# A two-layer hybrid transformer on one core: the residual stream kept with tokens on the partitions

## The chip, the cores and the metric

The kernel runs on one core of one Trainium2 chip. The metric is the device time of one execution in microseconds (us). A core has TensorE (PE in the rows; its weight loads are PEld), VectorE (DVE), ScalarE (ACT), GpSimd (POOL) and SyncE (SP), which here only issues DMAs. Each engine works through its own queue in order.

## The reference, cut to what matters

Two layers work on a residual `h` of 256 tokens by 2048 features, in float32. Each layer adds three branches to it: a mixer (two kinds of sparse attention in layer 0, a retention in layer 1), a cross-attention over 256 memory tokens, and a gated feed-forward of width 5632 with a short convolution. Every branch reads a normalised copy of `h` and ends in an output projection.

```python
for l in range(DEPTH):                       # DEPTH = 2
    hn = _rmsnorm(h, norm_mix[l])
    h = h + (_mixer_ab(hn, ...) if l % 2 == 0 else _mixer_c(hn, ...))   # ends in "@ w_out", K = 2048 and 4096
    h = h + _cross_attn(_rmsnorm(h, norm_cross[l]), mem_n, w_q[l], w_kv[l], w_o[l])   # "@ w_o", K = 512
    h = h + _conv_ffn(_rmsnorm(h, norm_ffn[l]), w_up[l], conv_w[l], conv_b[l], w_down[l])   # "@ w_down", K = 5632
return _rmsnorm(h, norm_final)

def _rmsnorm(x, g):
    return x * rsqrt(mean(x * x, axis=-1) + eps) * g
```

## The kernel before

**Numbers.** A float32 product is made of three matmuls in the fast float32 format: each operand is split in a high part and the rest (`hi` and `lo` of a weight, left and right half of an x tile), and hi·hi, hi·lo and lo·hi are summed in PSUM. `weights` (L225 to L239) loads 512 KB of a weight into one of 4 `raw` tiles (DMA on SP's queue), ScalarE makes `hi` (L235), VectorE makes `lo` (L236); a *slab* is 128 rows of the contraction.

**Two forms of product.** `product_b` (L241 to L287) holds the weights stationary and streams x: per slab and 128 output features one matmul over 512 columns (L275: hi times both halves of x) and one over 256 (L280: lo times x's high half). The result has features on the partitions and tokens along the row. `product_a` (L307 to L328) holds x stationary and streams the weights: per slab and 128 tokens three matmuls over the weight's columns (L323 to L325); the result has tokens on the partitions. `product_n` (L294 to L305) is the first form with three matmuls of 256 columns into a smaller PSUM tile; it serves the output projection of the cross-attention.

**The residual** lies with features on the partitions: `hT[s]` (L342 to L343), 16 tiles of 128 features by 256 tokens. All output projections use the first form in blocks of 256 features. `residual` (L595 to L604) adds a block's PSUM to `hT` with two VectorE additions (L598, L600) for each 128 features. In a branch's last projection `feed` (L345 to L349) at once makes that slab of the next branch's x (ScalarE L200, VectorE L203) and adds the slab's squares to a running sum (ScalarE L150, VectorE L151). The norm's scale per token follows from that sum: two tiny matmuls (L172), some 13 tiny VectorE operations (L178 to L189) and a broadcast by two matmuls (L196). The scale is applied behind the next branch's first products, so these do not wait for it.

**Order.** Engine queues are laid out by a scheduler from the order of the program, but where `manual_schedule` names TensorE, its queue is the program's order word for word. That holds for the mixer of layer 0, the cross-attention up to `w_o`, and the retention's heads. `run` advances generators that each yield after a few slabs and calls `pump`, which advances the generators in `side` (attention heads, the norm's scale, the memory's preparation) by one step.

**The end.** `final` (L1051 to L1061) scales each 128 features, turns them to tokens by two TensorE transposes (L1060) and copies them out; the last norm's scale is applied before the store.

Of the kernel before, what the change touches and what calls it, by code (L numbers as in the profile page):

```python
# [12 lines left out]
F32 = mybir.dt.float32  # L13
# [4 lines left out]
ALU = mybir.AluOpType  # L18
# [16 lines left out]
for _name, _n in (("mix", 32), ("cross", 32), ("mem", 16), ("ffn", 32), ("final", 16), ("gn", 32), ("pe_k", 32),  # L35
                  ("pe_v", 32), ("conv0", 352), ("conv1", 352)):
    PAR[_name] = (PAR_END, PAR_END + _n)
    PAR_END += _n


def cols(c0, c1, n):
# [34 lines left out]
def hybrid_kernel(ctx: ExitStack, tc: tile.TileContext, a, out):  # L76
# [61 lines left out]
    class Norm:  # L138


        def __init__(self):
            self.acc = None

        def add(self, h):
            if self.acc is None:
                self.acc = new([P, S], F32, "nacc", 2)
                act.activation(self.acc, h, AF.Square)
            else:
                sq = work()
                act.activation(sq, h, AF.Square)  # L150
                dve.tensor_add(self.acc, self.acc, sq)  # L151

        def row_steps(self):

            self.r = new([P, S], F32, "rstd", 2)
            yield
            yield
            self.c = rsqrt_col(self.acc, D)
            yield
            yield  # L160
            act.activation(self.r, on_rows(self.c), AF.Copy)

        def row(self):
            for _ in self.row_steps():
                pass
            return self.r
# [127 lines left out]
    def product_n(w, xs, c0, evac):  # L294

        b = bank()
        n = len(xs)
        ws = list(weights(w, 0, n, c0, 2 * P))
        for j in range(2):
            o, c = b[:, j * S : (j + 1) * S], slice(j * P, (j + 1) * P)  # L300
            for k, (hi, lo) in enumerate(ws):
                xh, xl = xs[k][:, 0:S], xs[k][:, S:]
                pe.matmul(o, hi[:, c], xh, start=(k == 0), stop=False)  # L303
                pe.matmul(o, hi[:, c], xl, start=False, stop=False)  # L304
                pe.matmul(o, lo[:, c], xh, start=False, stop=(k == n - 1))  # L305
        for j in range(2):
            evac(j, b[:, j * S : (j + 1) * S])  # L307

# [4 lines left out]
    def product_a_steps(w, xs, c0, ncol, evac):  # L313
        ws = weights(w, 0, len(xs), c0, ncol)
        acc = acc_tile()
        n = len(xs)
# [28 lines left out]
    def feed(norm, xs, g):  # L345
        def f(s):
            xs.append(xhat(hT[s], g[:, s : s + 1]))
            norm.add(hT[s])
        return f  # L349
# [3 lines left out]
    xs_mix = []  # L353
    held = [[], []]
# [10 lines left out]
    with tc.manual_schedule(engines=engines):  # L365
# [5 lines left out]
        for i in range(5):  # L371
            if i < 4:
# [8 lines left out]
                for k in range(4):  # L381
# [3 lines left out]
                    xhat_hi(xs_mix[s], hT[s], g)  # L385
# [3 lines left out]
                    xhat_lo(xs_mix[s], hT[s], g)  # L389
# [24 lines left out]
    def setup_steps():  # L414
# [7 lines left out]
        load_par(pool, "conv0", "conv1")  # L422

# [109 lines left out]
    def cross(l, xs, norm, head_done):  # L533
        region = ExitStack()
        region.enter_context(tc.manual_schedule(engines={mybir.EngineType.PE}))
# [19 lines left out]
        run(*[product_b_steps(weights(w_q, 0, ND, 2 * P * blk, 2 * P), xs, ev_q) for blk in range(2)])  # L555
# [5 lines left out]
        os, vs = [None] * 4, {}  # L561

        def head(h):
# [9 lines left out]
            while h // 2 not in vs:  # L573
                yield
            v, c = vs[h // 2], h % 2 * P
            o = bank()
            for kb in range(2):
                pe.matmul(o[:, 0:S], v[:, kb, c : c + P], pt[:, kb * S : (kb + 1) * S], start=(kb == 0), stop=(kb == 1))
# [5 lines left out]
        for blk in range(2):  # L584
            v = long().rearrange("p (t c) -> p t c", t=2)
            product_a(w_kv, xm, 512 + blk * 2 * P, 2 * P,
                      lambda t, acc: act.activation(v[:, t, :], acc, AF.Copy, scale=mem_rms[1][:, t : t + 1]), n=4)
            vs[blk] = v
        while side:
            pump(4)  # L590
        region.close()
# [259 lines left out]
    def ffn(l, xs, norm, done):  # L851
        row = norm.row()
# [3 lines left out]
        def convolved(acc, j):  # L856
# [6 lines left out]
            dve.tensor_mul(u[:, 2:], t, row)  # L863
# [6 lines left out]
        def up(s0, n):  # L870
            os = []
            for pair in range(n // 2):
# [14 lines left out]
                product_b(w_up, xs, j0 * P, ev_gate)  # L887
# [13 lines left out]
    def mixer_c(xs, norm, done):  # L901
        row, col = norm.row(), norm.c
# [3 lines left out]
        dve.tensor_mul(cos_r, cos_l[1], row)  # L906
        dve.tensor_mul(sin_r, sin_l[1], row)
# [15 lines left out]
        def head(h):  # L923
# [6 lines left out]
            def ev_v(t, acc):  # L930
                sm = small(1)
                act.activation(v[t], acc, AF.Identity, scale=col[:, t : t + 1], accum_out=sm)
# [7 lines left out]
            def ev_g(j, acc):  # L940
                u = work()
                into(u, acc, row)
# [56 lines left out]
        for hp in range(RET_HEADS // 2):  # L999
            with tc.manual_schedule(engines={mybir.EngineType.PE}):  # L1000
                os = head(2 * hp) + head(2 * hp + 1)
# [5 lines left out]

    n_cross = Norm()
    xs_c = []
# [10 lines left out]
    def mix_out(blk, os):  # L1020
        w = Weight("w_out_ab", D)
        ws = chain(weights(w, 8, 8, blk * 2 * P, 2 * P), weights(w, 0, 8, blk * 2 * P, 2 * P))
        return product_b_steps(ws, os, residual(2 * blk, fc), n=ND)

    with tc.manual_schedule(engines={mybir.EngineType.PE}):
        os = Ordered(*mixer_ab(xs_mix, row, col, kcv))
        fc = feed(n_cross, xs_c, gain("cross"))
        run(mix_out(0, os), mix_out(1, os))
    assert not side
    side.extend((angle_steps(1), mem_rms_steps()))  # L1030
    for blk in range(2, ND // 2):
        run(mix_out(blk, os))

    n_ffn = Norm()
    xs_f = []
    cross(0, xs_c, n_cross, feed(n_ffn, xs_f, gain("ffn")))
    n_mix = Norm()
    xs_m = []
    ffn(0, xs_f, n_ffn, feed(n_mix, xs_m, gain("mix")[:, ND:]))

    n_cross = Norm()
    xs_c = []
    mixer_c(xs_m, n_mix, feed(n_cross, xs_c, gain("cross")[:, ND:]))
    n_ffn = Norm()
    xs_f = []
    cross(1, xs_c, n_cross, feed(n_ffn, xs_f, gain("ffn")[:, ND:]))


    n_fin = Norm()
    fin = {}  # L1050

    def final(s):
        n_fin.add(hT[s])
        y = work()
        act.activation(y, hT[s], AF.Copy, scale=gain("final")[:, s : s + 1])
        b = bank()
        for t in range(2):
            if s % 4 == 0:
                fin[t, s // 4] = new([P, 512], F32, "xs", 32)
# [93 lines left out]
```

## Time and profile before

| what | value |
|---|---|
| median of 3 runs | 2885.48 us (2885.35 to 2887.01) |
| the profiled execution, its own time | 2888.33 us |
| its span, first to last instruction | 2886.6 us |
| TensorE busy | 2850.2 us, 99% of the span, 16434 matmuls |
| VectorE, ScalarE busy | 2095.7 us (73%), 1492.1 us (52%) |
| mean DMA rate | 183 GB/s, 527 MB in all |
| granted TensorE clock, mean | 0.996 |

The span is 1.7 us shorter than the execution's own time, and that time lies 2.85 us above the median of the runs. Matmuls overlap, so a row's mean duration is not what one costs: the distance between two starts is. In the rows of the timeline the columns are start, length, engine, line, operation, tiles and shape, count, and in brackets the idle time of the engine before it and what ended it.

### The profile page before, as it was taken

Reading aid. Unit: us, or ns where it says so; the run is one execution under the profiler, and the core shown is the slowest. Engines: PE = TensorE matmul, PEld = TensorE weight load, DVE = VectorE, ACT = ScalarE, POOL = GpSimd, SP = SyncE. Lnnn points to the kernel's source line nnn. Section 1 sums busy time; section 2 is a strip of 40 time slices with the busy share of each in tenths; the row PEclk is TensorE's granted clock in tenths of the full one; section 3 lists DMA queues with packets and bytes.
Section 4 is the critical chain, followed back from the end, with each engine's and each line's share of the span. In section 5 each row is a group of like instructions: output and inputs, shape, how many; then the busy total and the mean of one; then the engine's idle time right before and its main releaser. Section 6 shows DMA issues by size and latency. Waiting matters only on the chain.

```text
span 2886.6 us, 43866 instructions
## 1 busy us (share of the span) xinstructions
PE 2850.2 (99%) x16434; PEld 2508.4 (87%) x16434; DVE 2095.7 (73%) x3785; ACT 1492.1 (52%) x2274; POOL 27.1 (1%) x203
## 2 busy tenths in 40 slices
PE   9999999999999999999999999999999999999998
PEld 8888888988888888888888888888898888888886
DVE  7766786877777777786666667668777777777775
ACT  5344555654555455454444444445565454545555
POOL 0000000000000000000000000000000000000000
PEclk9999999999999999999999999999999999999999
DMA  8434555555555555655555555555555556565553
GB/s 283 155 124 139 170 194 186 175 190 184 183 194 190 187 190 192 192 189 177 179 182 180 187 177 183 175 180 188 190 173 189 187 180 196 188 191 189 189 188 123
DMA packets 155957, 527.26 MB, mean 183 GB/s; under 512 B 16928, under 2 KB 25536, under 8 KB 155744
## 3 DMA queue, kind: packets, MB, share of 16 engines
q1 hardware_dynamic: 154464, 521.55, 55.3%
q8 instruction: 129, 2.11, 0.3%
q0 software_dynamic: 704, 1.85, 0.2%
q10 hardware_dynamic: 576, 1.05, 0.1%
q14 instruction: 84, 0.69, 0.1%
HBM read 522.29 MB, written 2.10 MB: 182 GB/s over the span
## 4 chain that ended last, share of the span: by engine, by line
PE 93%; DVE 3%; DMA 1%; ACT 1%; issue 1%; SPq 0%; ACTq 0%; DVEq 0%
PE acc L275 51%; PE acc L280 26%; PE acc L323 3%; PE acc L325 3%; PE acc L324 3%; DVE t L236 1%; PE bank L964 0%; PE bank L675 0%; PE bank L479 0%; PE bank L303 0%; PE bank L305 0%; PE bank L304 0%; DMA t<-in_w_out_ab_dram 0%; PE bank L499 0%; PE bank L491 0%
## 5 line engine op out<-in xcount | busy, mean ns | idle before, releaser
L275 PE MATMUL acc<-t,t 128*128 128x512 f32 x6784 | 1645.0, 393 | 10.3 <-DVE t L203 6.5
L275 PEld LDWEIGHTS acc<-t,t 128*128 128x128 f32 x6784 | 1246.0, 189 | 252.6 <-DVE t L203 7.0
L235 ACT ACTIVATE t<-t 128x1024 fp32r<-128x1024 f32 x978 | 1018.0, 1042 | 817.1 <-PE acc L275 513.1
L236 DVE TENSOR_TENSOR t<-t,t 128x1024 fp32r<-128x1024 f32 x978 | 1174.8, 1203 | 352.0 <-ACT t L235 342.8
L280 PEld LDWEIGHTS acc<-t,t 128*128 128x128 f32 x6784 | 877.0, 191 | 42.0 <-DVE t L236 4.1
L280 PE MATMUL acc<-t,t 128*128 128x256 f32 x6784 | 897.2, 284 | 6.0 <-DVE t L236 3.6
L598 DVE TENSOR_TENSOR t<-t,acc 128x256 f32<-128x256 f32 x272 | 113.2, 416 | 108.0 <-PE acc L275 107.3
L323 PE MATMUL acc<-t,t 128*128 128x512 f32 (+2 forms) x512 | 181.6, 355 | 0.4 <-DVE t L335 0.4
L859 ACT ACTIVATE t<-acc 128x256 f32<-128x256 f32 x176 | 65.9, 374 | 220.1 <-PE acc L275 220.1
L325 PE MATMUL acc<-t,t 128*128 128x512 f32 (+2 forms) x512 | 179.3, 350 | 0.0
L324 PE MATMUL acc<-t,t 128*128 128x512 f32 (+2 forms) x512 | 179.2, 350 | 0.0
L862 DVE TENSOR_TENSOR t<-acc,t 128x256 f32<-128x256 f32 x176 | 74.1, 421 | 144.5 <-ACT t L859 144.5
L865 ACT ACTIVATE t<-t,t 128x256 f32<-128x256 f32 x176 | 106.0, 602 | 41.5 <-DVE t L863 41.2
L600 DVE TENSOR_TENSOR t<-t,acc 128x256 f32<-128x256 f32 x272 | 113.1, 416 | 4.1
L333 ACT ACTIVATE t<-acc 128x256 f32<-128x256 f32 x112 | 42.5, 380 | 133.2 <-PE acc L275 130.6
L323 PEld LDWEIGHTS acc<-t,t 128*128 128x128 f32 x512 | 96.8, 189 | 13.3 <-PE acc L280 0.5
L325 PEld LDWEIGHTS acc<-t,t 128*128 128x128 f32 x512 | 96.8, 189 | 12.6
L324 PEld LDWEIGHTS acc<-t,t 128*128 128x128 f32 x512 | 96.9, 189 | 12.2
L335 DVE TENSOR_TENSOR t<-acc,t 128x256 f32<-128x256 f32 x112 | 46.8, 418 | 66.1 <-ACT t L333 66.1
L867 DVE SCALAR_TENSOR_TENSOR t<-t,t,t 128x256 f32<-128x256 f32 x176 | 84.4, 479 | 2.8
L866 DVE SCALAR_TENSOR_TENSOR t<-t,t,t 128x256 f32<-128x256 f32 x176 | 84.2, 478 | 2.4 <-ACT t L865 1.5
L863 DVE TENSOR_TENSOR t<-t,t 128x256 f32<-128x256 f32 x176 | 74.4, 423 | 3.0
(195 smaller groups left out, 1396.1 us busy)
## 6 DMA issues: line engine op xcount, KB each, us to landing
t<-in_w_up_dram SPq DMA_DIRECT2D x352, 512.0 KB, 3.5
t<-in_w_in_c_dram SPq DMA_DIRECT2D x192, 512.0 KB, 3.7
t<-in_w_down_dram SPq DMA_DIRECT2D x160, 512.0 KB, 3.5
t<-in_w_in_ab_dram SPq DMA_DIRECT2D x83, 512.0 KB, 3.6
t<-in_w_out_c_dram SPq DMA_DIRECT2D x64, 512.0 KB, 3.6
t<-in_w_out_ab_dram SPq DMA_DIRECT2D x32, 512.0 KB, 4.4
t<-in_w_kv_x_dram SPq DMA_DIRECT2D x32, 512.0 KB, 4.1
t<-in_w_q_x_dram SPq DMA_DIRECT2D x16, 512.0 KB, 4.4
```

Of the source, the lines that this page charges most:

```text
L235: act.activation(hi[:, 0 : m * ncol], raw[:, 0 : m * ncol], AF.Copy)
L236: dve.tensor_sub(lo[:, 0 : m * ncol], raw[:, 0 : m * ncol], hi[:, 0 : m * ncol].bitcast(F32))
L275: pe.matmul(acc[:, j, :], parts[k - k0][0][:, j * P : (j + 1) * P], xs[k], start=(k == 0), stop=(end and k == n - 1))
L280: pe.matmul(acc[:, j, 0:S], parts[k - k0][1][:, j * P : (j + 1) * P], xs[k][:, 0:S], start=False, stop=(end and k == n - 1))
L323: pe.matmul(o, xh, hi, start=(k == 0), stop=False)
L324: pe.matmul(o, xh, lo, start=False, stop=False)
L325: pe.matmul(o, xl, hi, start=False, stop=(k == n - 1))
L598: dve.tensor_add(h, h, acc[:, 0:S])
L600: dve.tensor_add(h, h, acc[:, S:])
L865: act.activation(c, u[:, 2:], AF.Identity, bias=cp[:, 3, j : j + 1], scale=cp[:, 2, j : j + 1])
L866: dve.scalar_tensor_tensor(c, u[:, 1 : S + 1], cp[:, 1, j : j + 1], c, op0=ALU.mult, op1=ALU.add)
L867: dve.scalar_tensor_tensor(c, u[:, 0:S], cp[:, 0, j : j + 1], c, op0=ALU.mult, op1=ALU.add)
```

## The change

1. The residual is held with tokens on the partitions: `res[t]`, two tiles of 128 tokens by 2048 features, loaded from a second copy of the input (`rows`, 2 MB) by two DMAs on SP's queue. The first norm still reads the input with features on the partitions, whose tiles now come from the pool `long`.
2. All output projections use the second form (x stationary) over 512 columns, and so does the value projection of the cross-attention, which had 256. `product_n` is gone. A group of 512 output features has one addition for each 128 tokens.
3. A norm's squares are summed by ScalarE's accumulating output (8 numbers per token), so VectorE's running sum and the two tiny matmuls go.
4. Where a group is final, a generator `turn(g)` goes into `side`: two steps later it transposes the group's 4 slabs by 8 TensorE transposes and makes the next x from PSUM.
5. The end needs no transposes: it multiplies by the gain laid out along the row (`gains`, 4 DMAs on POOL's queue).
6. TensorE's queue is the program's order from the first mixer to the end; the scales of the norms before the feed-forward and the retention become `side` steps.

```diff
 WIDTHS = {
...
-    "w_kv_x": cols(0, 1024, 256),
-    "w_out_ab": cols(0, D, 256),
-    "w_out_c": cols(0, D, 256),
-    "w_o_x": cols(0, D, 256),
-    "w_down": cols(0, D, 256),
+    "w_kv_x": cols(0, 512, 256) + [(512, 512)],
+    "w_out_ab": cols(0, D, 512),
+    "w_out_c": cols(0, D, 512),
+    "w_o_x": cols(0, D, 512),
+    "w_down": cols(0, D, 512),
 }
...
         def __init__(self):
-            self.acc = None
-
-        def add(self, h):
-            if self.acc is None:
-                self.acc = new([P, S], F32, "nacc", 2)
-                act.activation(self.acc, h, AF.Square)
-            else:
-                sq = work()
-                act.activation(sq, h, AF.Square)
-                dve.tensor_add(self.acc, self.acc, sq)
+            self.sq = new([P, 8], F32, "sq", 2)
+
+        def add(self, t, g):
+            junk = new([P, 512], F32, "p", 7)
+            act.activation(junk, part(t, g), AF.Square, accum_out=self.sq[:, 4 * t + g : 4 * t + g + 1])
+
+        def column(self):
+            v = small(2)
+            dve.tensor_reduce(v, self.sq.rearrange("p (t i) -> p t i", t=2), axis=AX.X, op=ALU.add)
+            self.c = rsqrt_of(v, D)
+            return self.c
...
-    x_in = [new([P, 2, S]) for _ in range(ND // 2)]
-    hT = [x_in[s // 2][:, s % 2, :] for s in range(ND)]
+    res = [new([P, D]) for _ in range(2)]
+
+    def part(t, g):
+        return res[t][:, 512 * g : 512 * g + 512]
+
+    def feed(norm, xs, gains):
+        def turn(g):
+            yield
+            yield
+            for s in range(4 * g, 4 * g + 4):
+                b = bank()
+                for t in range(2):
+                    pe.transpose(b[:, t * P : (t + 1) * P], res[t][:, s * P : (s + 1) * P], ident)
+                xs[s] = xhat(b[:, 0:S], gains[:, s : s + 1])
+
+        def f(g):
+            for t in range(2):
+                norm.add(t, g)
+            side.append(turn(g))
...
+        for t in range(2):
+            nc.sync.dma_start(res[t], a["rows"][t * P : (t + 1) * P, :])
...
-        for blk in range(ND // 2):
-            product_n(w_o, os, blk * 2 * P, residual(2 * blk, head_done))
-
-    def residual(s0, done=None):
-        def ev(j, acc):
-            h = hT[s0 + j]
-            dve.tensor_add(h, h, acc[:, 0:S])
-            if acc.shape[-1] > S:
-                dve.tensor_add(h, h, acc[:, S:])
-            if done is not None:
-                done(s0 + j)
+        out_product(w_o, os, 0, head_done)
+
+    def residual(g, done=None):
+        def ev(t, acc):
+            dve.tensor_add(part(t, g), part(t, g), acc)
+            if t and done is not None:
+                done(g)
         return ev
 
     def out_product(w, xs, s0, done=None):
-        for blk in range(ND // 2):
-            product_b(w, xs, blk * 2 * P, residual(2 * blk, done), s0=s0)
+        for g in range(4):
+            run(product_a_steps(w, xs, 512 * g, 512, residual(g, done), s0=s0))
...
     def ffn(l, xs, norm, done):
-        row = norm.row()
+        side.append(norm.row_steps())
...
+        def final(g):
+            for t in range(2):
+                norm.add(t, g)
+                ys[t, g] = new([P, 512], F32, "xs", 32)
+                dve.tensor_mul(ys[t, g], part(t, g), gains[g])
```

How the queues move shows at three places. **SP's queue near the start** (t is a tile, `in_w_in_ab` the first mixer's weights, `in_cmp_w_k` a table that the first mixer needs later). Before:

```order
L234 DMA t_383<-in_w_in_ab_dram 128x1024
L234 DMA t_442<-in_w_in_ab_dram 128x1024
L656 DMA t_513<-in_cmp_w_k_dram 128x4x128
L656 DMA t_515<-in_cmp_w_k_dram 128x4x128
L656 DMA t_517<-in_cmp_w_k_dram 128x4x128
L234 DMA t_473<-in_w_in_ab_dram 128x1024
```

Now:

```order
L229 DMA t_385<-in_w_in_ab_dram 128x1024
L229 DMA t_444<-in_w_in_ab_dram 128x1024
L421 DMA t_72<-in_rows_dram 128x2048
L421 DMA t_73<-in_rows_dram 128x2048
L229 DMA t_477<-in_w_in_ab_dram 128x1024
L646 DMA t_517<-in_cmp_w_k_dram 128x4x128
```

The two loads of `rows`, 1 MB each, stand ahead of that product's third and fourth weight loads; the fourth follows the eighth table load, as it did before.

**TensorE's queue where the cross-attention ends and the feed-forward begins** (bank is a PSUM bank, t_72 and t_73 the residual, t_61 the identity, acc_5210 the first product of `w_up`). Before, the last row of `w_o` and the first of `w_up` were neighbours:

```order
L305 MATMUL bank_5516<-t_5198,t_5519 128x256
L275 MATMUL acc_5588<-t_5234,t_5590 128x512 x2
L275 MATMUL acc_5588<-t_5240,t_5590 128x512 x2
L275 MATMUL acc_5588<-t_5278,t_5590 128x512 x2
L275 MATMUL acc_5588<-t_5285,t_5590 128x512 x2
```

Now the last group's transposes stand between the second and the third four slabs of `w_up`:

```order
L270 MATMUL acc_5210<-t_5139,t_5256 128x512 x2
L337 MATMUL bank_5277<-t_61,t_72 128x128
L337 MATMUL bank_5277<-t_61,t_73 128x128
L337 MATMUL bank_5283<-t_61,t_72 128x128
L337 MATMUL bank_5283<-t_61,t_73 128x128
L337 MATMUL bank_5289<-t_61,t_72 128x128
L337 MATMUL bank_5289<-t_61,t_73 128x128
L337 MATMUL bank_5295<-t_61,t_72 128x128
L337 MATMUL bank_5295<-t_61,t_73 128x128
L270 MATMUL acc_5210<-t_5188,t_5302 128x512 x2
```

So a group has two steps of the next product (32 matmuls, 16 of each length) between its last matmul and its transposes, and the x made of it is read one step (16 matmuls) behind them.

**VectorE's queue where the first cross-attention begins** (t_4378 is the fourth load of memory features, t_4388 and the like the weights of `w_q`). Before, twelve of the sixteen L203 rows on the memory stood ahead of the norm's scale (L178):

```order
L203 SCALAR_TENSOR_TENSOR t_4484<-t_4473,t_71,t_4484 128x256
L178 TENSOR_SCALAR t_4454<-bank_4451 128x2
L236 TENSOR_TENSOR t_4489<-t_4487,t_4488 128x1024
L180 TENSOR_SCALAR t_4456<-t_4454 128x2
L203 SCALAR_TENSOR_TENSOR t_4511<-t_4509,t_71,t_4511 128x256
```

Now twelve stand behind the scale and behind the last group's x (L198 on a bank):

```order
L184 SCALAR_TENSOR_TENSOR t_4224<-t_4235,t_4224 128x2
L198 SCALAR_TENSOR_TENSOR t_4279<-bank_4276,t_71,t_4279 128x256
L198 SCALAR_TENSOR_TENSOR t_4285<-bank_4282,t_71,t_4285 128x256
L198 SCALAR_TENSOR_TENSOR t_4291<-bank_4288,t_71,t_4291 128x256
L198 SCALAR_TENSOR_TENSOR t_4297<-bank_4294,t_71,t_4297 128x256
L198 SCALAR_TENSOR_TENSOR t_4302<-t_4300,t_71,t_4302 128x256
```

Eleven more such rows follow, then the `lo` of the fifth weight load of `w_q` (L231), which TensorE reads 32 matmuls of each length, eight transposes and two broadcasts after the last group.

## Rows read from the trace of the kernel before

**Rows 1.** The page's part 4, the chain that ended last.
```profile
PE 93%; DVE 3%; DMA 1%; ACT 1%; issue 1%; SPq 0%; ACTq 0%; DVEq 0%
```
**Rows 2.** Timeline of TensorE in a stretch of products with stationary weights.
```profile
847.92 3.82 PE L275 MATMUL acc<-t,t 128*128 128x512 f32 x16
...
853.49 3.82 PE L275 MATMUL acc<-t,t 128*128 128x512 f32 x16
```
**Rows 3.** Timeline of TensorE in a value product of the retention, x stationary.
```profile
1367.41 0.39 PE L323 MATMUL acc<-t,t 128*128 128x512 f32 x1
...
1373.54 0.39 PE L323 MATMUL acc<-t,t 128*128 128x512 f32 x1
```
**Rows 4.** Timeline of TensorE in the cross-attention's output projection.
```profile
513.25 0.28 PE L303 MATMUL bank<-t,t 128*128 128x256 f32 x1
...
514.33 0.28 PE L303 MATMUL bank<-t,t 128*128 128x256 f32 x1
```
**Rows 5.** Timeline of TensorE around six transposes of attention weights.
```profile
341.74 0.82 PE L479 MATMUL bank<-t,t 128*128 128x128 f32 x6
342.31 2.09 PE L275 MATMUL acc<-t,t 128*128 128x512 f32 x8
```
**Rows 6.** Windows: the last projection's stretch with transposes, for L275, then for L280.
```profile
2828.40:2871.60 43.20, 27.07 (x105) 18.61 (x104) 1.00 0.28 88
...
2828.40:2871.60 43.20, 18.04 (x112) 15.51 (x111) 1.00 0.28 88
```
**Rows 7.** Timeline of TensorE around a norm's tiny matmuls.
```profile
1333.09 0.50 PE L172 MATMUL bank<-t,t 128*128 128x1 f32 x4
1333.45 0.72 PE L275 MATMUL acc<-t,t 128*128 128x512 f32 x2
```
**Rows 8.** Timeline of TensorE: its long waits outside the feed-forward, and what followed.
```profile
349.53 0.78 PE L280 MATMUL acc<-t,t 128*128 128x256 f32 x4 [2.39 <-ACT t L213]
350.15 3.51 PE L275 MATMUL acc<-t,t 128*128 128x512 f32 x8
...
445.08 0.71 PE L196 MATMUL bank<-t,t 128*128 128x128 f32 x4 [3.54 <-DVE t L189]
...
2032.24 1.45 PE L280 MATMUL acc<-t,t 128*128 128x256 f32 x8 [1.58 <-DVE t L236]
```
**Rows 9.** Windows behind the second of them (granted clock: third number from the end).
```profile
445.00:448.80 3.80, 3.72 (x12) 3.06 (x13) 2.39 (x3) 1.33 (x2) 0.00 (x0) 0.61 0.67 204
```
**Rows 10.** Lines by form: all 512-column matmuls; idle time before them by what ended it.
```profile
L275 PE MATMUL acc<-t,t 128*128 128x512 f32 x6784 | 1645.0, 393 | 10.3 <-DVE t L203 6.5 <-DVE t L600 3.2 <-DVE t L335 0.6
```
**Rows 11.** Windows of the start (last two numbers: share of the DMA engines, GB/s).
```profile
10.00:20.00 10.00, 10.00 (x53) 8.84 (x52) 8.61 (x16) 9.42 (x17) 0.00 (x0) 1.00 1.01 389
...
30.00:40.00 10.00, 9.64 (x78) 9.31 (x77) 7.63 (x24) 4.16 (x7) 0.00 (x0) 1.00 1.04 337
```
**Rows 12.** Timeline of ScalarE, then of TensorE, at the first mixer's fourth weight load.
```profile
37.78 1.98 ACT L235 ACTIVATE t<-t 128x1024 fp32r<-128x1024 f32 x2 [2.64 <-DMA t<-in_w_in_ab_dram]
...
42.24 0.36 PE L323 MATMUL acc<-t,t 128*128 128x256 f32 x1
```
**Rows 13.** Lines by form: VectorE's and ScalarE's operations that the change adds or drops.
```profile
L236 DVE TENSOR_TENSOR t<-t,t 128x1024 fp32r<-128x1024 f32 x940 | 1147.4, 1222 | 351.3 <-ACT t L235 342.1 <-PE bank L704 0.6 <-ACT t L1061 0.4
L598 DVE TENSOR_TENSOR t<-t,acc 128x256 f32<-128x256 f32 x272 | 113.2, 416 | 108.0 <-PE acc L275 107.3
L203 DVE SCALAR_TENSOR_TENSOR t<-t,t,t 128x256 fp32r<-128x256 f32 x128 | 58.4, 477 | 1.2 <-ACT t L200 1.2
L236 DVE TENSOR_TENSOR t<-t,t 128x512 fp32r<-128x512 f32 x32 | 21.9, 683 | 0.7 <-ACT t L235 0.7
L932 ACT ACTIVATE t<-acc,t 128x512 f32<-128x512 f32 x16 | 10.9, 685 | 13.4 <-PE acc L325 13.4
```
**Rows 14.** Timeline of VectorE at the end: first of the last additions, first step of the scale.
```profile
2871.59 0.42 DVE L598 TENSOR_TENSOR t<-t,acc 128x256 f32<-128x256 f32 x1 [3.69 <-PE acc L275]
...
2875.23 0.16 DVE L178 TENSOR_SCALAR t<-bank 128x2 f32<-128x2 f32 x1 [1.01 <-PE bank L172]
```

More of the change, by code (lines that the diff above doesn't have):

```diff
@@ L353, in hybrid_kernel @@
     xs_mix = []
+    x_in = [long().rearrange("p (s t) -> p s t", t=S) for _ in range(ND // 2)]
     held = [[], []]
@@ L554, in cross @@
         side.extend((norm.row_steps(), mem_steps()))
-        run(*[product_b_steps(weights(w_q, 0, ND, 2 * P * blk, 2 * P), xs, ev_q) for blk in range(2)])
+        run(*[product_b_steps(weights(w_q, 0, ND, 2 * P * blk, 2 * P), xs, ev_q) for blk in range(2)], n=4)
         def ev_k(j, acc):
@@ L1018, in __getitem__, with stage, mix_out @@
             return self.os[self.order[k]]
-    def mix_out(blk, os):
+    def stage(gains):
+        norm, xs = Norm(), [None] * ND
+        return norm, xs, feed(norm, xs, gains)
+    def mix_out(g, os, done):
         w = Weight("w_out_ab", D)
-        ws = chain(weights(w, 8, 8, blk * 2 * P, 2 * P), weights(w, 0, 8, blk * 2 * P, 2 * P))
-        return product_b_steps(ws, os, residual(2 * blk, fc), n=ND)
-    with tc.manual_schedule(engines={mybir.EngineType.PE}):
-        os = Ordered(*mixer_ab(xs_mix, row, col, kcv))
-        fc = feed(n_cross, xs_c, gain("cross"))
-        run(mix_out(0, os), mix_out(1, os))
@@ L1029, in hybrid_kernel @@
[L1029 to L1046, printed above, removed]
@@ L1049, in hybrid_kernel @@
[L1049 to L1059, printed above, removed]
-            pe.transpose(b[:, t * P : (t + 1) * P], y[:, t * P : (t + 1) * P], ident)
-            act.activation(fin[t, s // 4][:, s % 4 * P : (s % 4 + 1) * P], b[:, t * P : (t + 1) * P], AF.Copy)
@@ L1063, in hybrid_kernel @@
[L1063 to L1072 removed]
+        ws = chain(weights(w, 8, 8, g * 512, 512), weights(w, 0, 8, g * 512, 512))
@@ new lines, in mix_out, with layers @@
+        return product_a_steps(None, os, 0, 512, residual(g, done), ws=ws, n=ND)
+    def layers():
+        os = Ordered(*mixer_ab(xs_mix, row, col, kcv))
+        norm, xs, done = stage(gain("cross"))
+        run(mix_out(0, os, done), mix_out(1, os, done))
+        assert not any(x is None for x in os.os)
+        side.extend((angle_steps(1), mem_rms_steps()))
+        for g in range(2, 4):
+            run(mix_out(g, os, done), n=4)
+        n_ffn, xs_f, done = stage(gain("ffn"))
+        cross(0, xs, norm, done)
+        n_mix, xs_m, done = stage(gain("mix")[:, ND:])
+        ffn(0, xs_f, n_ffn, done)
+        norm, xs, done = stage(gain("cross")[:, ND:])
+        mixer_c(xs_m, n_mix, done)
+        n_ffn, xs_f, done = stage(gain("ffn")[:, ND:])
+        cross(1, xs, norm, done)
+        norm = Norm()
+        gains = [long() for _ in range(4)]
+        for g in range(4):
+            pool.dma_start(gains[g], a["norm_final"][g * 512 : (g + 1) * 512].partition_broadcast(P))
+        ys = {}
+        def final(g):
[3 more added lines that the diff above has]
+                dve.tensor_mul(ys[t, g], part(t, g), gains[g])
+        ffn(1, xs_f, n_ffn, final)
+        c = norm.column()
+        for g in range(4):
+            for t in range(2):
+                y = ys[t, g]
+                if t == 0:
+                    dve.tensor_scalar_mul(y, y, c[:, t : t + 1])
+                else:
+                    act.activation(y, y, AF.Copy, scale=c[:, t : t + 1])
+                (nc.sync if t == 0 else act).dma_start(out[0, t * P : (t + 1) * P, g * 512 : (g + 1) * 512], y)
```

91 lines of the change are left out of this document (27 added, 64 removed).

## The prediction

> **What bounds the kernel now.** The first view is the chain that ended last: TensorE makes up 93% of it [rows 1], so a microsecond counts only if it shortens TensorE's queue, a wait of TensorE, or what stands ahead of its first and behind its last matmul. VectorE at 73% and ScalarE at 52% are off the path except where TensorE waits for them. The second view is the timeline of TensorE, for the price of a matmul. With stationary weights 16 matmuls of 512 columns and 16 of 256 repeat every 853.49 - 847.92 = 5.57 us, 0.348 a pair [rows 2]; with x stationary 27 matmuls of 512 take 6.13 us, 0.227 each [rows 3]; nine of 256 take 1.08 us, 0.120 each [rows 4]. So 256 more columns cost 0.107 us, the pace of 2.4 GHz, and 0.013 us come with every matmul whatever its width: the same columns in fewer matmuls are cheaper, by little. The third view is the list of waits; TensorE has few, and each long one costs twice: 2.39 and 3.54 us of idling are each followed by matmuls at half pace (eight of 512 columns in 3.51 us [rows 8], against 2.09 in rows 5), with a granted clock of 0.61 in the 3.8 us behind the second, that is partly at 1.2 GHz [rows 9]. I call this echo 1.5 us.
>
> **The change, part by part** (minus is a gain).
>
> *Projections of the mixers and the feed-forward.* Per slab and 512 features, four pairs (4 x 0.348 = 1.392) become six matmuls (6 x 0.227 = 1.362) [rows 2, 3]. There are 16 slabs in the first mixer, 32 in the second, 44 in each feed-forward, times four groups: 544 units x 0.030 = -16.5.
>
> *Output and value projections of the cross-attention.* Twelve matmuls of 256 (1.440 [rows 4]) become six of 512 (1.362): 64 units x 0.078 = -5.0.
>
> A rule speaks against these two terms. By rows 2 to 4 a matmul costs 0.013 us beside its columns. The Trainium skill ("TensorE: Matmul & The Clock Gate", section "Back-to-back issue gap") gives columns / 2.4 GHz plus 2.5 ns for a warm engine. By that rule both terms together would be an estimated -3.7 in place of -21.5, and the whole sum would end 3 us above the time before. The trace disagrees, 227 and 120 ns against the rule's 216 and 109, so the sum goes by the rows.
>
> *Transposes added.* Five stages times four groups times eight. Six cost 342.31 - 341.74 = 0.57 us of TensorE's time [rows 5], so eight cost 0.76 to 0.80; I take 0.78: +15.6.
>
> *Transposes removed.* In the last projection 105 pairs and 7 more short matmuls should take 37.4 us and took 43.2 [rows 6]: -5.8.
>
> *Norm sums.* The four short passes of L172 hold TensorE for 0.36 us [rows 7]; five such places lie ahead of the end: -1.8. VectorE and ScalarE change too (two additions of about 0.68 per group, from the 512-column row, in place of eight of 0.416 [rows 13]; eight squarings of 0.685 in place of sixteen of 0.4), all beside TensorE's work except as told below.
>
> *The copy of the input.* 2.10 MB go through SP's queue at 23 us, where the DMA engines are busy throughout (share 1.04 at 337 GB/s, up to 389 [rows 11]), so all that stands behind comes 5.4 to 6.2 us later. The fourth weight load came at 37.7, its `hi` and `lo` took 2.2 and TensorE read them at 42.24 [rows 12]: 2.2 us of cover, so a new wait of 3.2 to 4.0. Below lies nothing (earlier requests could make it up), above 4.0 and an echo. I take 3.3 + 1.5 = +4.8. The 4 loads of `gains` on POOL's queue are hidden behind a whole feed-forward.
>
> *Waits that go.* In the first mixer's projection TensorE idled 2.39 us for ScalarE, which was held by a memory load [rows 8]; with groups twice as wide that load is issued behind eight more weight loads. With the echo this is -3.8. In its place the last heads' softmax now shares VectorE with the steps of an angle table; a wait of 0 to 3.8, I take 1.5: -2.3. In the feed-forward TensorE waited 3.2 us in all for additions (L600) that free a PSUM buffer [rows 10]; a group now takes twice as long until its buffer is wanted again, and is read by two operations: -3.2.
>
> *Start of the two cross-attentions.* Before, 3.54 and 1.58 us of waiting [rows 8], each with an echo: 8.1. Now VectorE makes the twelve later memory tiles behind the last group's x. From that group's last matmul: its transposes end at 2 x 2.8 + 0.8 = 6.4; four L203 of 0.477 bring 8.3, twelve 14.0, the fifth `lo` (1.22) 15.2 [rows 13], while TensorE wants it at 4 x 2.8 + 0.9 = 12.1: 3.1 us and an echo twice, 9.2. Overlapped starts would make it 7.4. Against 8.1 I take 0; bounds -8 (no wait left) and +8 (raw buffers come late on top).
>
> *Other starts.* At the feed-forward and the retention the additions (2 x 0.68, behind at most two 1.22 of VectorE) are through 4 us after the group, the transposes come at 5.6: hidden. Without that cover a turn would wait 1 to 2 us.
>
> *The end.* From the last addition's start to the scale's first step, 3.64 us now [rows 14]. Then two additions, two multiplications (4 x 0.68) and a reduction of 0.16: 2.9. -0.7.
>
> **Sum.** -16.5 - 5.0 + 15.6 - 5.8 - 1.8 + 4.8 - 2.3 - 3.2 + 0 - 0.7 = -14.9. Against the profiled execution's 2888.33 that gives 2873.4; this execution lay 2.85 above the median of the runs, so the median should come to 2870.6, say 2871, 0.5% faster. A measurement of this kernel can tell about 0.2%, 5.8 us, from no change.
>
> **The rivals.**
>
> *The cross-attentions start without a wait* (2863). For it: ScalarE and VectorE do less per slab ahead of it, and the scale's chain starts earlier. Against: the queue shows twelve memory tiles ahead of the weight that TensorE wants.
>
> *Some transposes wait* (about 2879). TensorE's queue is now fixed, and a turn that stands ahead of its additions blocks it. In the cross-attention's projection VectorE has 2 x 1.22 + 4 x 0.477 + 2 x 0.68 = 5.7 us of work per group [rows 13], TensorE 24 x 0.227 + 0.78 = 6.2 [rows 3, 5]: hardly room. Eight such turns with 1 us each make +8.
>
> *Slower: the turns wait with an echo* (2896). The same place, once VectorE falls behind for good: each of the eight turns then idles about 1.6 us and wakes at half pace, 8 x 3.1 = +25. It decides from 2.6 us per turn (14.9 + 5.8 over eight), or 1.04 us if all twenty wait. Against it: the cover of 5.4 us between a group's end and its turn.
>
> *No gain per matmul* (2888 to 2892). The 0.013 us may belong to the loading of a new stationary operand as x and weights alternate, not to the count of matmuls, and then the new products pay it elsewhere: without the -21.5 the sum is +6.6, with the rule above +3. Against it: rows 3 measured this very form.
>
> **How the numbers follow.** The forecast within 6 us (2865 to 2877) has 0.59, the waitless starts 0.13, some waits 0.15 (a third of it still faster by over 0.2%), waits with an echo 0.07, no gain per matmul 0.06. Faster by over 0.2%: 0.59 + 0.13 + 0.05 = 0.77. Within 0.2%: 0.10 + 0.05 = 0.15. Slower: 0.07 + 0.01 = 0.08. The range 2860 to 2886 takes in the first three cases with the bounds of the copy and of the starts and leaves out 0.13 to 0.16.
>
> **What would show it.** Right: 0.227 us between the matmuls of all output projections; each of the twenty turns 0.78 us with no idle time ahead; a new wait near 43 us with ScalarE's `hi` ended by a weight load; one wait of 2 to 4 us at each cross-attention, at the fifth or sixth weight load of `w_q`; no wait for L590 in the feed-forward. Wrong: TensorE idle ahead of L337, a pace other than 0.227, or a wait in the middle of a stage.

## The result and the profile after

| | before | after |
|---|---|---|
| median of 6 runs | 2886.89 us (2885.35 to 2888.74) | 2866.21 us (2864.91 to 2867.21) |
| ratio | | 0.9928, 95% interval 0.9915 to 0.9941 |
| span of the profiled execution | 2886.6 us | 2864.8 us |

The change takes 20.7 us off. The forecast was 14.9 off and 2871, with a range of 2860 to 2886. The profiled spans differ by 21.8 us. The page of the kernel after, parts 1 and 4, answers to [rows 1]:

```profile
PE 2830.5 (99%) x15066; PEld 2439.5 (85%) x15066; DVE 1966.0 (69%) x3269; ACT 1469.0 (51%) x2206; POOL 29.5 (1%) x207
...
PE 96%; ACT 1%; DVE 1%; DMA 1%; issue 0%; SPq 0%; ACTq 0%
```

TensorE holds still more of the chain, with 1368 matmuls fewer. To see where the time went, both traces are cut where the first matmul of the next projection starts. "Forecast" puts the prediction's own terms on these stretches (a group's turn counts where it stands: three of four in the stretch that makes them, the last in the next; the 0 for the starts of the cross-attentions is 0 at each).

| stretch | before | after | difference | forecast |
|---|---|---|---|---|
| start to the first `w_out_ab` | 326.06 | 332.51 | +6.5 | +4.8 |
| first mixer's output projection | 99.38 | 96.17 | -3.2 | -1.9 |
| first cross-attention | 108.93 | 104.52 | -4.4 | +0.2 |
| first feed-forward | 738.46 | 733.33 | -5.1 | -4.2 |
| retention | 748.87 | 747.31 | -1.6 | -1.1 |
| second cross-attention | 105.72 | 105.44 | -0.3 | +0.2 |
| second feed-forward and the end | 759.18 | 745.52 | -13.7 | -13.0 |

Every stretch but the first came out better than forecast, and only one by more than 1.4 us: the first cross-attention.

The lists of TensorE's waits add up to 25.2 us before and 19.5 after, and between the products the granted clock fell to its lower level, 1.2 GHz, behind three waits before and behind one after, at about 1.7 us of lost time each. So some 9 us of the 21.8 are waits and what followed them; the rest is the products, the transposes and the end.

**The pace of a matmul.** Timeline of TensorE after, in the last `w_down`, which answers to [rows 2, 3] (the columns are those told above):

```profile
2839.73 0.39 PE L303 MATMUL acc<-t,t 128*128 128x512 f32 x1
...
2849.70 0.39 PE L305 MATMUL acc<-t,t 128*128 128x512 f32 x1
```

Between these rows lie 44 steps: 9.97 / 44 = 0.227 us, as in [rows 3].

**A turn.** Timeline of TensorE after, at the last group of the first mixer:

```profile
434.24 1.04 PE L337 MATMUL bank<-t,t 128*128 128x128 f32 x8
435.03 1.19 PE L275 MATMUL acc<-t,t 128*128 128x256 f32 x8
```

The next product is 0.79 us behind the first transpose, with no idle time ahead of it. Nineteen of the twenty turns look like this. The other one, 4.7 us behind its forerunner in the first mixer, idles 0.88 for a PSUM bank that VectorE (L198) still reads.

**What TensorE waits for.** Waits of the kernel after, TensorE alone (what is waited for, total us, times, longest):

```profile
PE acc L270 <- DVE t L198: 7.1, 2, 6.9
PE acc L304 <- DVE t L231: 2.3, 1, 2.3
PE acc L270 <- ACT t L230: 1.9, 2, 1.0
PE acc L270 <- DVE t L315: 1.9, 2, 1.4
PE acc L303 <- ACT t L230: 1.6, 1, 1.6
PE bank L574 <- ACT t L581: 1.6, 2, 0.8
PE bank L478 <- DVE t L470: 1.3, 3, 0.9
PE bank L337 <- DVE t L198: 0.9, 1, 0.9
```

The 6.9 of the first row is the wait for the first matmul. No row names L590: no PSUM buffer waits for an addition any more (3.2 us in [rows 10]), and no turn for its additions.

**The new wait at the start.** Timeline of ScalarE, then of TensorE, after, where [rows 12] stood:

```profile
43.01 0.38 ACT L616 ACTIVATE t<-bank 128x256 f32<-128x256 f32 x1 [6.14 <-PE bank L191]
43.43 1.97 ACT L230 ACTIVATE t<-t 128x1024 fp32r<-128x1024 f32 x2
```

```profile
44.54 0.38 PE L303 MATMUL acc<-t,t 128*128 128x256 f32 x1 [1.56 <-ACT t L230]
47.22 0.39 PE L304 MATMUL acc<-t,t 128*128 128x256 f32 x1 [2.30 <-DVE t L231]
```

ScalarE starts the fourth `hi` at 43.43 instead of 37.78: the load landed at 43.34, 5.6 us later than before. TensorE idles 1.56 us for `hi` and then 2.30 for `lo`, which VectorE makes behind other work. Windows after, behind this wait (third number from the end: granted clock):

```profile
47.00:54.00 7.00, 6.78 (x42) 6.78 (x43) 6.17 (x11) 2.15 (x4) 0.00 (x0) 0.76 0.68 205
```

Seven microseconds at a mean of 0.76, so partly at the lower level, 1.2 GHz, are another 7 x 0.24 = 1.7.

**The starts of the cross-attentions.** Timeline after of TensorE, of VectorE and of ScalarE at the first one:

```profile
439.30 2.00 PE L270 MATMUL acc<-t,t 128*128 128x512 f32 x8
442.27 2.11 PE L270 MATMUL acc<-t,t 128*128 128x512 f32 x8 [0.97 <-ACT t L230]
444.22 1.11 PE L275 MATMUL acc<-t,t 128*128 128x256 f32 x8
...
454.20 2.08 PE L270 MATMUL acc<-t,t 128*128 128x512 f32 x8 [0.48 <-DVE t L315]
```

```profile
436.74 5.05 DVE L198 SCALAR_TENSOR_TENSOR t<-t,t,t 128x256 fp32r<-128x256 f32 x12
442.25 2.36 DVE L231 TENSOR_TENSOR t<-t,t 128x1024 fp32r<-128x1024 f32 x2 [0.46 <-ACT t L230]
```

```profile
439.16 2.11 ACT L195 ACTIVATE t<-t,t 128x256 fp32r<-128x256 f32 x5
441.17 2.00 ACT L230 ACTIVATE t<-t 128x1024 fp32r<-128x1024 f32 x2
```

Instead of 3.54 us [rows 8] TensorE waits 0.97 for the fifth `hi`, and 0.48 later on. At the second start, after:

```profile
2027.43 2.11 PE L270 MATMUL acc<-t,t 128*128 128x512 f32 x8 [0.97 <-ACT t L230]
...
2040.28 2.09 PE L270 MATMUL acc<-t,t 128*128 128x512 f32 x8 [1.40 <-DVE t L315]
```

That is 2.4 us, where there had been 1.58 and an echo. Windows behind the two waits of 0.97 show the full clock:

```profile
442.00:446.00 4.00, 3.73 (x20) 3.27 (x21) 2.54 (x3) 2.23 (x3) 0.00 (x0) 1.00 0.92 287
...
2027.40:2031.00 3.60, 3.57 (x19) 3.13 (x20) 2.49 (x3) 1.99 (x2) 0.00 (x0) 1.00 0.88 312
```

**The end.** Timeline of VectorE after, which answers to [rows 14]:

```profile
2850.13 1.28 DVE L590 TENSOR_TENSOR t<-t,acc 128x512 f32<-128x512 f32 x2 [7.25 <-PE acc L305]
...
2852.72 0.17 DVE L173 TENSOR_SCALAR t<-t 128x2 f32<-128x2 f32 x1
```

From the last addition's start to the scale's first step 2.59 us, where it had been 3.64.

### The profile page after: what moved, and what is told of

Same layout as the page of the kernel before. It is cut to its first block, busy times and chain, and to the rows that moved or that the text cites. A ratio compares the mean times of both kernels' runs of the same rounds, so it can differ in the third digit from the quotient of the medians.

```text
span 2864.8 us, 40356 instructions
## 1 busy us (share of the span) xinstructions
PE 2830.5 (99%) x15066; PEld 2439.5 (85%) x15066; DVE 1966.0 (69%) x3269; ACT 1469.0 (51%) x2206; POOL 29.5 (1%) x207
## 3 DMA queue, kind: packets, MB, share of 16 engines
q8 instruction: 118, 1.93, 0.3%
q10 hardware_dynamic: 576, 1.05, 0.1%
## 4 chain that ended last, share of the span: by engine, by line
PE 96%; ACT 1%; DVE 1%; DMA 1%; issue 0%; SPq 0%; ACTq 0%
PE acc L270 36%; PE acc L275 19%; PE acc L303 12%; PE acc L304 12%; PE acc L305 12%; PE bank L337 1%; PE bank L958 0%; PE bank L665 0%; PE bank L478 0%; PE bank L498 0%; ACT t L195 0%; PE bank L490 0%; DVE t L231 0%; ACT t L230 0%; PE bank L574 0%
## 5 line engine op out<-in xcount | busy, mean ns | idle before, releaser
L231 DVE TENSOR_TENSOR t<-t,t 128x1024 fp32r<-128x1024 f32 x962 | 1172.8, 1221 | 544.8 <-ACT t L230 535.4
L270 PE MATMUL acc<-t,t 128*128 128x512 f32 x4608 | 1117.3, 392 | 11.7 <-DVE t L198 7.1
L270 PEld LDWEIGHTS acc<-t,t 128*128 128x128 f32 x4608 | 844.3, 189 | 176.1 <-DVE t L198 7.9
L303 PE MATMUL acc<-t,t 128*128 128x512 f32 (+2 forms) x1600 | 621.2, 388 | 1.7 <-ACT t L230 1.6
L304 PE MATMUL acc<-t,t 128*128 128x512 f32 (+2 forms) x1600 | 616.8, 386 | 2.3 <-DVE t L231 2.3
L305 PE MATMUL acc<-t,t 128*128 128x512 f32 (+2 forms) x1600 | 617.0, 386 | 0.0
L275 PEld LDWEIGHTS acc<-t,t 128*128 128x128 f32 x4608 | 593.7, 191 | 24.1 <-DVE t L390 0.5
L275 PE MATMUL acc<-t,t 128*128 128x256 f32 x4608 | 608.3, 283 | 0.0
L303 PEld LDWEIGHTS acc<-t,t 128*128 128x128 f32 x1600 | 301.3, 188 | 61.6 <-ACT t L230 1.8
L304 PEld LDWEIGHTS acc<-t,t 128*128 128x128 f32 x1600 | 301.4, 188 | 61.0 <-DVE t L231 2.5
L305 PEld LDWEIGHTS acc<-t,t 128*128 128x128 f32 x1600 | 301.1, 188 | 60.4
L590 DVE TENSOR_TENSOR t<-t,acc 128x512 f32<-128x512 f32 x152 | 97.6, 683 | 31.7 <-PE acc L305 31.6
L315 DVE TENSOR_TENSOR t<-acc,t 128x256 f32<-128x256 f32 x112 | 46.8, 418 | 64.2 <-ACT t L313 64.2
L869 ACT ACTIVATE t<-t 128x256 f32<-128x256 f32 x88 | 36.0, 409 | 24.7 <-DVE t L857 24.7
```

What stands on the lines that cost most here:

```text
L231: dve.tensor_sub(lo[:, 0 : m * ncol], raw[:, 0 : m * ncol], hi[:, 0 : m * ncol].bitcast(F32))
L270: pe.matmul(acc[:, j, :], parts[k - k0][0][:, j * P : (j + 1) * P], xs[k], start=(k == 0), stop=(end and k == n - 1))
L275: pe.matmul(acc[:, j, 0:S], parts[k - k0][1][:, j * P : (j + 1) * P], xs[k][:, 0:S], start=False, stop=(end and k == n - 1))
L303: pe.matmul(o, xh, hi, start=(k == 0), stop=False)
L304: pe.matmul(o, xh, lo, start=False, stop=False)
L305: pe.matmul(o, xl, hi, start=False, stop=(k == n - 1))
```

## The experiments

All are edits of the changed kernel; "changed" is its median, 2866.2. The versions ran on several chips, where the kernel before came out at 2885.97 to 2887.21 beside them, so a difference of one or two microseconds is read against that kernel too.

### Later loads of the input's copy

```diff
-        for t in range(2):
-            nc.sync.dma_start(res[t], a["rows"][t * P : (t + 1) * P, :])
...
         for quad in range(2):
+            if quad == 1:
+                for t in range(2):
+                    dve.tensor_copy(res[t][:, 0:1], v[t][:, 0:1])
+                    nc.sync.dma_start(res[t], a["rows"][t * P : (t + 1) * P, :])
             v = [long(), long()]
```

> The changed kernel, but the two loads of `rows` are issued some 150 us later, in the first mixer's second half (two one-column copies on VectorE hold them back until then). Theory: in the changed kernel TensorE idles 1.56 and 2.30 us near 44 us, since the fourth weight load lands at 43.34 instead of 37.70, and the granted clock behind it is 0.65 and 0.84 for 7 us, another 1.7 us. All of that goes: 3.9 + 1.7 = 5.6 us off 2866.2, so 2860.6, and the fourth load lands before 38. Rival: the start is bound by the sum of all loads, so what is not waited for here is waited for a few us later: within 1 us of 2866.

2860.78 us (2860.09 to 2861.28): 5.4 below the changed kernel, ratio to before 0.9909 (0.9895 to 0.9924). The timelines of ScalarE and TensorE of this version:

```profile
37.84 1.06 ACT L230 ACTIVATE t<-t 128x1024 fp32r<-128x1024 f32 x1 [1.83 <-DMA t<-in_w_in_ab_dram]
```

```profile
41.88 0.60 PE L191 MATMUL bank<-t,t 128*128 128x128 f32 x4
42.24 0.36 PE L303 MATMUL acc<-t,t 128*128 128x256 f32 x1
```

Its windows, where the clock had been 0.76:

```profile
47.00:54.00 7.00, 7.00 (x57) 7.00 (x56) 6.90 (x17) 2.44 (x4) 0.00 (x0) 1.00 1.01 305
```

Now issued at 181 and 186 us, the two loads leave the start alone: the `hi` starts at 37.84, TensorE goes on without a wait at 42.24 (the same time as in [rows 12]) at full clock, and the first `w_out_ab` starts at 326.11, in the kernel before at 326.06. So the whole loss of the first stretch was the place of these two loads. The rival, a start bound by the sum of the loads, is out.

### Each transpose twice

```diff
-                for t in range(2):
+                for t in (0, 1, 0, 1):
                     pe.transpose(b[:, t * P : (t + 1) * P], res[t][:, s * P : (s + 1) * P], ident)
```

> The changed kernel, but each turn makes its transposes twice (the second time over the first's result). It prices them. Theory: they lie on the path in full, 20 turns x 0.79 us (the distance from a turn's first transpose to the next product's matmul in the profile after) = +15.8, and at the two cross-attentions the x of the last group comes 0.8 later, at most +1.6: 2882 to 2884. Rival: some turns stand where TensorE would wait anyway, for the additions or for x, and cost nothing there: under +12, below 2878.

2884.9 us (2883.51 to 2885.93), +18.7. Timeline of TensorE at the turn shown above:

```profile
434.81 1.91 PE L337 MATMUL bank<-t,t 128*128 128x128 f32 x16
436.48 0.72 PE L275 MATMUL acc<-t,t 128*128 128x256 f32 x4
```

Sixteen take 1.67 us, so the second eight cost 0.88: 20 x 0.88 = 17.6, and the rest is within the runs' spread and the later x: in this trace the wait for L315 at the first cross-attention has grown from 0.48 to 2.24 us, and the clock falls behind it. The first eight cost less (0.79), as a product's first matmul follows the last transpose closely. Transposes lie on the path in full: the price taken in the prediction stands. So the gross gain of the change is some 36 us (20.7 + 15.8, an estimate), of which its transposes take 15.8.

### The transposes right behind their group

```diff
         def turn(g):
-            yield
-            yield
+            if g < 0:
+                yield
```

> The changed kernel without the two steps between a group and its turn: the transposes stand right behind the group's last matmul. It tries the rival that ends slower. By the profile after, the second addition of a group ends 1.7 us after TensorE has finished issuing the group, so each of the 20 turns idles TensorE 1.7 us. Theory: each of them also wakes at the low clock and pays an echo of 1.2 to 1.5 us, as the wait of 1.58 us in the kernel before did: 20 x 3.0 = +60, 2925. Rival: a wait so short costs itself only: 20 x 1.7 = +34, 2900. Third: VectorE takes the additions earlier, and there is no wait at all: 2866.

2897.68 us (2897.47 to 2898.28), slower than before: ratio 1.0038 (1.0023 to 1.0053). That is +31.5 on the changed kernel, 1.57 a turn. Timeline of TensorE at one of them, and a window behind it:

```profile
1246.55 0.33 PE L337 MATMUL bank<-t,t 128*128 128x128 f32 x1 [0.78 <-DVE t L590]
1247.15 0.98 PE L337 MATMUL bank<-t,t 128*128 128x128 f32 x7 [0.27 <-DVE t L590]
1247.88 0.48 PE L303 MATMUL acc<-t,t 128*128 128x512 f32 x1
```

```profile
1250.00:1254.00 4.00, 4.00 (x19) 3.31 (x18) 1.37 (x2) 1.39 (x2) 0.00 (x0) 1.00 0.22 89
```

TensorE waits for each of the two additions in turn, 1.05 us together, and from the start of the group's last matmul to the next product it takes 2.51 us where it took 1.02. The clock stays at 1.00 behind this turn and behind eighteen others: no echo. Only the second turn, which waited 1.93 us for its first addition, has one. That wait, and the window behind it:

```profile
385.17 0.33 PE L337 MATMUL bank<-t,t 128*128 128x128 f32 x1 [1.93 <-DVE t L590]
```

```profile
387.10:390.40 3.30, 3.30 (x9) 2.56 (x8) 3.07 (x8) 1.78 (x4) 0.00 (x0) 0.50 0.85 268
```

The slower rival's mechanism exists, but it costs some 1.6 us a turn, and not the 3.1 the prediction gave it. The place of the transposes, two steps on, hides all of it.

### `w_down` in blocks of 256 columns

```diff
-    "w_down": cols(0, D, 512),
+    "w_down": cols(0, D, 256),
...
-    def out_product(w, xs, s0, done=None):
+    def out_product(w, xs, s0, done=None, n=512):
         for g in range(4):
-            run(product_a_steps(w, xs, 512 * g, 512, residual(g, done), s0=s0))
+            for c in range(0, 512, n):
+                run(product_a_steps(w, xs, 512 * g + c, n, residual(g, done, c, n), s0=s0))
```

> The changed kernel, but `w_down` goes in blocks of 256 columns: 12 matmuls of 256 in place of 6 of 512 per slab and 512 features, the same columns, twice the matmuls and weight loads, and four additions of 0.42 in place of two of 0.68. It prices a matmul beside its columns. Theory (rows of the kernel before, 120 against 227 ns): 2 layers x 44 slabs x 4 groups x (12 x 0.120 - 6 x 0.227 = 0.078) = +27.5, 2893.7. Rival, the Trainium skill's rule ("TensorE: Matmul & The Clock Gate", section "Back-to-back issue gap"), 2.5 ns a matmul: 2112 more matmuls, an estimated +5.3, 2871.5.

2894.64 us (2892.11 to 2896.85), +28.4. Timeline of TensorE of this version:

```profile
1227.05 0.28 PE L303 MATMUL acc<-t,t 128*128 128x256 f32 x1
...
1229.93 0.28 PE L303 MATMUL acc<-t,t 128*128 128x256 f32 x1
```

24 steps in 2.88 us are 0.120 each. The same columns in twice the matmuls cost 28.4 / 2112 = 0.0134 us more per matmul, as [rows 2 to 4] had it (0.013); by these paces alone it is 352 x 0.078 = 27.5. The rule of the Trainium skill ("TensorE: Matmul & The Clock Gate", section "Back-to-back issue gap"), a formula that the section gives for an isolated matmul, made it an estimated +5.3; here the measurement decides against it. Every matmul here loads its own weights, so whether the 0.013 belongs to the matmul or to the load was not told apart.

### One step ahead of a turn instead of two

```diff
         def turn(g):
             yield
-            yield
```

> The changed kernel with one step instead of two between a group and its turn. By the profile after, a turn's transposes start 3.85 to 4.98 us behind the end of the last addition (18 of 20 turns); one step less takes 12 x 0.227 = 2.7 off, so 1.1 to 2.2 are left. Theory: TensorE still waits for no addition, and the x of the last group comes 2.7 earlier at the two cross-attentions, so their waits of 0.97 (for ScalarE's `hi` of the fifth `w_q` load) go: -2 to -3, 2863 to 2864. Rival: the scheduler leaves the twelve memory tiles where they are, and the start keeps its waits: 2866. Third: the margin is too small, turns wait: over 2870.

2869.06 us (2868.47 to 2872.89), +2.9 (+3.6 when each version is taken against the kernel before beside it): a miss. The median lies between the rival's 2866 and the third case, over 2870, and the third case's cause is not there: no turn waits for an addition. Timelines of TensorE and VectorE of this version at the first cross-attention:

```profile
440.24 1.22 PE L275 MATMUL acc<-t,t 128*128 128x256 f32 x8 [1.99 <-DVE t L231]
```

```profile
432.36 1.66 DVE L198 SCALAR_TENSOR_TENSOR t<-bank,t,t 128x256 fp32r<-128x256 f32 x4
...
435.39 3.65 DVE L198 SCALAR_TENSOR_TENSOR t<-t,t,t 128x256 fp32r<-128x256 f32 x9
438.96 1.23 DVE L231 TENSOR_TENSOR t<-t,t 128x1024 fp32r<-128x1024 f32 x1
```

Counted from the group's end, the x of the last group comes 2.5 us earlier, and with it the scheduler moves the memory tiles ahead: all twelve now stand before the `lo` of the fourth load, which in the changed kernel was made ahead of the scale. TensorE waits 1.99 for it and 1.15 for L315 behind it; the second start keeps 1.50 for ScalarE and 1.44 for L315, and the turn that waits for a PSUM bank waits 1.40 instead of 0.88. Together that is 2.8 us more than in the changed kernel. An earlier x was of no use, as the queue behind it was re-ordered.

### Memory tiles two per step

```diff
                 for s in range(4):
                     xm.append(xhat(m[:, s * S : (s + 1) * S], gain("mem")[:, 4 * i + s : 4 * i + s + 1]))
-                yield
+                    if s % 2:
+                        yield
```

> The changed kernel, but the cross-attention's memory tiles are made two per step instead of four, so that fewer stand ahead of the fifth `w_q` load on ScalarE and VectorE (8 in place of 12, 4 x 0.42 us). Theory: the two waits of 0.97 us go, -1.9, and the waits of 0.48 and 1.40 behind them stay: 2864.3. Rival: what is not made here is made later, and the waits grow there (at the product of `w_kv`): 2866 or above.

2864.61 us (2863.71 to 2866.69), -1.6, or -0.85 when each version is taken against the kernel before beside it: less than the spread of the runs. Its list of TensorE's waits:

```profile
PE acc L270 <- DVE t L315: 3.1, 2, 1.6
...
PE acc L275 <- DVE t L231: 0.6, 1, 0.6
```

Both waits of 0.97 are gone, but 1.2 us of them come back at L315 (1.9 in the changed kernel) and 0.6 at a `lo`, so the two starts wait 3.7 us in all where they waited 3.8. The number agrees with the theory, but the trace shows the rival's mechanism (the waits grow further on), and no gain from the spread tiles is shown. L315 empties the PSUM buffer that the next product needs.

### Together

`joined` has the three edits above (late loads, one step, spread tiles), `late_spread` the late loads and the spread tiles.

> The changed kernel with the late loads of `rows`, one step ahead of a turn, and the memory tiles two per step, together. Theory: the first brings 5.4 as measured, the other two share one cause (waits at the two cross-attentions, 0.97 + 0.48 and 0.97 + 1.40 us in the profile after), so together at most 3.8: 2857 to 2859. Rival: the two undo each other (memory tiles now compete with the earlier x): 2861 or more.

2864.11 us (2861.28 to 2865.53): the rival's side, and no better than the late loads alone. Timeline of TensorE and window behind it, of `joined`:

```profile
449.64 2.73 PE L270 MATMUL acc<-t,t 128*128 128x512 f32 x8 [1.92 <-DVE t L315]
```

```profile
449.20:453.00 3.80, 3.36 (x12) 2.87 (x13) 3.38 (x7) 1.37 (x3) 0.00 (x0) 0.72 0.84 306
```

The wait for L315 has grown to 1.92 us (2.03 at the second start) and the clock falls behind both. This is the trace of the slowest of the five executions; two others came out at 2861.28 and 2861.64, so what the clock does there may be most of the difference, but no trace of theirs shows it.

> The changed kernel with the late loads of `rows` and the memory tiles two per step, but with two steps ahead of a turn again. Theory: the step taken out before a turn is what cost the joined version its gain (turns_one alone came out 2.9 above the changed kernel), so -5.4 and -1.6 as measured apart: 2859.2. Rival: the late copy and the spread tiles do not add up, as both leave the same waits for L315 at the two cross-attentions: 2861 or more.

2860.13 us (2858.97 to 2861.47), ratio to before 0.9911 (0.9897 to 0.9924): the lowest median, but not to be told from the late loads alone (2860.78, ratio 0.9909). So the step taken out cost the joined version some 4 us in the medians, in the trace above mostly by the two falls of the clock (about 1.7 us each), and the spread tiles add nothing that these runs show on top of the late copy. What is left at the cross-attentions hangs on L315.

### TensorE's order free again where it had been free

The wrap around `layers()` goes, and the three places named in the section on the kernel before get theirs back.

```diff
-    with tc.manual_schedule(engines={mybir.EngineType.PE}):
-        layers()
+    layers()
```

> The changed kernel with part 6 of the change undone: TensorE's queue is the program's order only where it was before, so the scheduler lays out the output projections, the feed-forward and the transposes in them. Theory: the turns' place in the program has 3.85 to 4.98 us behind their additions, so the fixed order prevents no wait and causes none: within 3 us of 2866.2. Rival: the scheduler puts transposes elsewhere, where they wait for additions or where their bank comes free late: 2870 or more.

2867.05 us (2865.3 to 2868.01): no difference. In both traces TensorE's instructions stand in the same sequence, by line and shape, so the scheduler laid out what the program fixes, and what another order would cost is not shown. The fixed order of part 6 is worth nothing by itself here; its other half, the scales as `side` steps, was not undone.

## Why the prediction was right

*The sum.* By the two traces, the terms without a wait (products, transposes, norm sums, the end) were forecast at -14.2 us and came to about -14.9. The waits with their echoes were forecast at -0.7 and came to about -6.8: the start +6.6 for +4.8, the first mixer's projection -4.1 for -2.3, the feed-forwards -3.3 for -3.2, the cross-attentions -6.0 for 0. So nearly all of the distance between forecast and result lies in the waits. These are estimates from the idle times and the granted clock of each stretch.

*Projections, -16.5 and -5.0: right, a little small.* Eight slabs of `w_out_c`, 32 units, took 44.64 us in the kernel before (1558.63 to 1603.27) and 43.52 after (1552.47 to 1595.99), 0.035 a unit; the eight-slab passes of `w_down` went from 44.53 to 43.52, 0.032 a unit. The prediction had 0.030, and 544 units at 0.032 to 0.035 are -17.4 to -19.0. That the gain goes with the count of matmuls, each with its weight load, is shown by the 256-column run; the rival "no gain per matmul" falls with the pace measured after.

*Transposes, +15.6: right.* 20 x 0.79 = 15.8, shown on the path by doubling them.

*Last transposes, -5.8, the end, -0.7, norm sums, -1.8: right together.* The last stretch came out at -13.7 for -13.0; 1.05 of that is the end, for 0.7.

*The copy of the input, +4.8: right in place and kind, too small.* The new wait was forecast near 43 us with ScalarE's `hi` late, 3.3 us and an echo of 1.5; it was 1.56 + 2.30 = 3.9 and 1.7. Taken away, it gave back 5.4 in the medians and 6.4 in the first stretch of the traces.

*Waits that go, -2.3 and -3.2: right.* The 2.39 us for a memory load is gone (with its echo of 1.5 that is 3.9, and not the 3.8 of the prediction). In its place the prediction put 1.5 for a softmax; what came is the 0.88 for a PSUM bank. The waits for additions (L600) are all gone.

*Starts of the cross-attentions, 0: the term that was mis-sized.* The step that failed is "the fifth `lo` 15.2, while TensorE wants it at 12.1". At about that time TensorE wants the fifth `hi`, and the `lo` only eight matmuls later. Counted from the last group's end at 428.68, it came to the fifth load at 442.27 - 0.97 = 441.30, so after 12.6, and without a wait it would have come to the `lo` 444.22 - 442.27 = 1.95 later, after 14.6. The twelve tiles took 5.05 us (0.42 each) and not 5.7, and the `lo`, the first of the two from 442.25, was through after 14.8. So `lo` alone would have been late by 0.2 us at most; the wait was for ScalarE's `hi`, which stood behind the same twelve tiles, and 0.97 us left no echo. Waits of 1.45 and 2.37 us, with no echo, came in place of the 8.1 before: -4.3 of the 5.1 by which the two stretches beat the forecast. The prediction also left out a wait of the kernel before, for the fourth `lo` at the first start, which is gone too. Timeline of TensorE before:

```profile
435.71 1.22 PE L280 MATMUL acc<-t,t 128*128 128x256 f32 x8 [1.40 <-DVE t L236]
```

With these 1.40 us the waits account for all of the 5.1 (the -6.0 above takes each echo at 1.7 and every wait of the two stretches). The result lies between the forecast and its rival "the cross-attentions start without a wait" (2863).

*Some transposes wait; turns wait with an echo: did not happen,* but for the 0.88 us at one turn, the prediction's own sign of "TensorE idle ahead of L337". The transposes start 3.85 to 4.98 us behind the end of their additions in 19 of 20 turns, and 3.44 in the other. The run without the two steps shows what they would have cost.

## What to carry to other kernels

Price a change of form by distances between starts in the trace, width by width: here 0.013 us per matmul beside its columns, times the count, paid for twenty groups of transposes and left a gain. When work is added to a full DMA queue, ask which load stands behind it and whether it could be issued where the queue has room: two loads moved from 24 us to 181 and 186 us were worth a quarter of the whole change. Before costing a late operand, look up which of its parts TensorE reads first, and keep in mind that an earlier input can re-order the queue that was to profit from it.

## What the runs showed of the chip that was not expected

The same idle time of TensorE is not followed by the same clock. Behind 1.58 us in the kernel before the granted clock was 0.63, behind 1.92 in `joined` 0.72 and behind 1.93 in the version without the two steps 0.50, yet behind 1.99 in the one-step version and behind a later wait of 2.17 in the version without the two steps it was 1.00. Windows behind the wait of 1.58 (kernel before), and behind that of 1.99 (one-step version):

```profile
2032.00:2036.00 4.00, 3.76 (x14) 3.23 (x15) 3.48 (x13) 2.98 (x5) 0.00 (x0) 0.63 0.89 285
```

```profile
440.20:444.00 3.80, 3.63 (x18) 2.87 (x19) 2.27 (x5) 2.28 (x5) 0.00 (x0) 1.00 0.88 274
```

So the echo that the prediction added to every wait of about 1.6 us or more is a possibility at that length, not a rule; waits of 1.4 us and less showed none in the stretches read here.
